# A two-layer attention / S5 diffusion step: the S5 scan tile laid out in runs of 8, x stored early, adaLN steps in pairs, 12 of them moved into S5

## The chip, the core and the metric

The kernel runs on one core of one Trainium2 chip. The metric is the device time of one execution in microseconds. Before the change the median of 3 runs is 2644.32 us (2640.66 to 2646.99). The engines of the core work side by side, each in its own program order: TensorE (PE, with PEld for its weight loads), VectorE (DVE), ScalarE (ACT), GpSimd (POOL) and SyncE (SP, which here only issues transfers).

## The reference, cut

Two token groups (128 context rows `xp`, 128 latent rows `xs`; D = 2048) pass two layers with shared weights. adaLN vectors come from a conditioning vector times a 2048 x 12288 matrix per layer. Layer 0 mixes by attention, layer 1 by a bidirectional diagonal state-space scan (S5) with a gate; a convolutional gated FFN follows each.

```python
for i in range(DEPTH):                      # 2 layers
    mp = ada_params(c_ctx[None, :], ada_w[i], ada_b[i])   # silu(cond) @ w + b, split in 6
    ms = ada_params(c, ada_w[i], ada_b[i])
    hp = rms_norm(xp, norm1_g[i]) * (1 + mp[1]) + mp[0]
    hs = rms_norm(xs, norm1_g[i]) * (1 + ms[1]) + ms[0]
    # i = 0: qkv, attention, w_o      i = 1: s5_mixer
    xp = xp + mp[2] * op; xs = xs + ms[2] * os_
    hp = rms_norm(xp, norm2_g[i]) * (1 + mp[4]) + mp[3]; ...
    xp = xp + mp[5] * conv_ffn(hp, *ffn); ...

def s5_mixer(h, h0, w_in, ..., w_gate, w_out):
    u = h @ w_in                            # 128 groups of 16 channels, 64 states each
    for d, rev in ((0, False), (1, True)):
        bu = einsum('blgc,gpc->blgp', u, bb)        # complex
        hs = associative_scan(abar, bu, reverse=rev)
        y += einsum('blgp,gcp->blgc', hs, c)        # real part
    y = gelu(y); y = y * sigmoid(y @ w_gate)
    return y @ w_out, final states
```

## The kernel before, in words

**Products.** Both token groups stand side by side as two blocks of 128 columns. A weight matrix is streamed from HBM in units of 128 x 1024 float32 (512 KB) by SP into 8 `raw` buffers (a few more in two stretches). A *split* unit is written by ACT as a rounded high part `whi` and by DVE as the remainder `wlo`, up to 3 units ahead; PE then runs 12 matmuls of 512 columns into two `acc` banks (`products`). The first three quarters of w_gate are not split: there PE takes the float32 `raw` directly (`acc<-raw`).

**adaLN steps.** `ada` returns four steps for 512 columns of one adaLN vector. A step takes two units (1 MB) and is four column-tiled float32 matmuls (32 columns of the array each) into the one `ada` bank. The profile records each as two matmuls, so one step is 8 records `ada<-raw,cond`. After the fourth step DVE adds the bias (`adab`, loaded by POOL) into `adaev`, PE transposes it, DVE reduces it to shift or scale columns (or PE and ACT make gate rows). The steps are needed late and are therefore strewn between the dense steps by `spread(main, fill)`, one at a time. 200 steps stand in the program.

**Order.** The program order is made by the code in `run_all`: after each unit `pump()` lets background tasks (attention, convolution, the S5 preparation and scan) put their next instructions into the streams when a planner's clock (`Timeline`) says that their operands are ready. The planner decides the order alone; each engine then runs its stream in order and waits on semaphores. The constants `EARLY` and `FILL` say how many adaLN steps of layer 1 stand in the first FFN (FFN0) and in S5 (in w_in and in the four quarters of w_gate).

**S5.** `w_in` makes u in four quarters q; `s5_prep` (POOL, during FFN0) makes the tables. For each q, `scan_task` multiplies u by the input tables (`ms<-A,A` 128x128), and ACT copies each PSUM bank into the scan tile `SC` (tag S0 for q = 0, 2; tag X for q = 1, 3): 16 copies of 64 x 512. SC holds 33 time steps of 128 values; in one step the values stand as [re/im][group][block]. `steps_task` makes 32 scan steps of 4 DVE instructions each. `out_task` lets ACT copy SC into two tiles `sf` (4 copies of 64 x 2048), PE multiplies these by the output tables (`ms<-A,A` 128x64, column-tiled in halves, 96 records for each of two tiles), ACT applies gelu, PE transposes, ACT copies into y; then the quarter's w_gate products run. Since q = 1 scans in the tile X, where the residual x lives, SP stores x to DRAM (`xd`) first and loads it again at the end.

Of the kernel before, what the change touches and what calls it, by code (L numbers as in the profile page):

```python
# [16 lines left out]
P = 128  # L17
# [20 lines left out]
EARLY = 20  # L38
# [3 lines left out]
FILL = (2, 0, 2, 2, 2)  # L42
# [27 lines left out]
class Timeline:  # L70
# [144 lines left out]
    def engine(self, eng, name, outs, ins, args, kw):  # L215
        n = max(math.prod(x.shape[1:]) for x in outs + ins)
        scal = sum(isinstance(kw.get(k), bass.AP) for k in ("scale", "bias", "scalar1", "scalar2"))
        big = [x for x in ins if math.prod(x.shape[1:]) > 1 or n == 1]
        scal += len([x for x in ins if math.prod(x.shape[1:]) == 1 and n > 1 and not any(x is kw.get(k) for k in ("scale","bias"))])
        if eng == "ACT":  # L220
            ps = self.in_psum(big[0])
            slow = 1.0
            for x in outs + big:
                st = [d for d in list(x.ap)[1:] if d[1] > 1]
                if st and abs(st[-1][0]) > 16: slow = 2.15
            c = (0.05 if ps else 0.095) + slow * n / 1200.0 + 0.09 * scal + 0.09 * ("accum_out" in kw)
# [12 lines left out]
        self.run(eng, c, outs, ins, name)
# [38 lines left out]
def spread(main, fill):  # L278
    out, j = [], 0
    for i, s in enumerate(main):  # L280
        out.append(s)
        while j < len(fill) and (j + 1) * len(main) <= (i + 1) * len(fill):
            out.append(fill[j])
            j += 1
    return out + fill[j:]
# [3 lines left out]
def hybrid_kernel(ctx: ExitStack, tc: tile.TileContext, a):  # L289
# [206 lines left out]
    def run_all():  # L496
# [13 lines left out]
        j = 0  # L510
        for u in units:
# [17 lines left out]
            pump()  # L529
# [816 lines left out]
    class S5:  # L1346
# [43 lines left out]
        def scan_task(self):  # L1390
# [8 lines left out]
            w1 = view(wt, 0, [[64, 2], [2, 32], [1, 2]])  # L1399
            w2 = view(wt, 128, [[64, 2], [2, 32], [1, 2]])  # L1400
            for q in range(4):
# [13 lines left out]
                gps.memset(SC[:, 0, :, :, 0], 0.0)  # L1415
                gps.tensor_copy(SC[:, 0, :, :, 1], s5par["H0"][:, :, 32 * q:32 * q + 32])
                for e2 in range(2):
                    e = 2 * q + e2
                    for h in range(2):
                        for ri in range(2):  # L1420
# [9 lines left out]
                            bw = view(SC, 32 * 128 + ri * 64 + g0, [[1, 16], [-128, 32]], (64, 64))  # L1430
# [6 lines left out]
                a_re = view(s5par["A4"], 32 * q, [[0, 2], [1, 32], [0, 2]])  # L1437
                a_im = view(s5par["A4"], G + 32 * q, [[G, 2], [1, 32], [0, 2]])
# [3 lines left out]
        def steps_task(self):  # L1442
            q = 0
            while q < 4:
# [3 lines left out]
                for s in range(32):  # L1448
                    cur = SC[:, s]
                    swp = view(SC, s * 128 + 64, [[-64, 2], [2, 32], [1, 2]])  # L1450
# [10 lines left out]
        def out_task(self):  # L1461
# [8 lines left out]
            for q in range(4):  # L1470
# [6 lines left out]
                gps.tensor_copy(fin[:, :, 32 * q:32 * q + 32], SC[:, 32, :, :, 0])  # L1477
# [172 lines left out]
    m = s5.w_in()  # L1650
    start_hook(ffn0.last_up, lambda: (spawn(s5.steps_task()), spawn(s5.scan_task()), spawn(s5.out_task())))
# [110 lines left out]
```

## Time and profile before

| | |
|---|---|
| median of 3 runs | 2644.32 us |
| profiled execution, own time | 2647.6 us |
| its span, first to last instruction | 2645.8 us |
| PE busy | 2545.2 us, 96% |
| DVE / ACT / POOL busy | 60% / 50% / 17% |
| TensorE clock granted, mean | 0.987 of full speed |
| chain of work that ended last | PE 86%, ACT 4%, DVE 4%, DMA 3% |
| HBM traffic | 651 MB, mean 246 GB/s |

Stages in the span: adaLN prologue to 24 us, qkv with attention to 389, w_o to 531, FFN0 to 1410, w_in 1417 to 1553, w_gate quarters 0 to 2 to 1725, w_gate quarter 3 and w_out to 1871, FFN1 to the end. An engine that is not the bottleneck may idle at no cost, so the busy share is read stage by stage: where PE never waits, the time of the stage is the sum of its matmuls.

### The profile page before, as it was taken

How to read it: one execution, taken by the hardware profiler on the slowest of the kernel's cores; microseconds unless marked ns; L12 is line 12 of the kernel's file. 1: busy time of each engine (PE TensorE's matmuls, PEld its weight loads, DVE VectorE, ACT ScalarE, POOL GpSimd, SP SyncE). 2: the span in 40 equal slices, each digit the busy share in tenths (PEclk: the TensorE clock that was granted, in tenths of full speed). 3: DMA queues.
4: the chain of work that ended last, by engine and by line, in shares of the span. 5: the costliest groups of instructions: out<-in, count | busy, mean ns of one | idle time of the engine just before them, and what ended most of it. 6: DMA issues, size and time to landing. Idle time of an engine off the chain costs nothing.

```text
span 2645.8 us, 35232 instructions
## 1 busy us (share of the span) xinstructions
PE 2545.2 (96%) x13011; PEld 1893.5 (72%) x13011; DVE 1599.1 (60%) x2370; ACT 1323.0 (50%) x1764; POOL 442.5 (17%) x455
## 2 busy tenths in 40 slices
PE   8999999999999999999998769999999999999998
PEld 4666677667777777777776655466677788888896
DVE  4765554567665665566656386655656565666566
ACT  5333444356554554455455668543555544554354
POOL 0002000011465555455530000000000000000000
PEclk9999999999999999999999889999999999999999
DMA  9979877977888888888886756789677756665663
GB/s 360 321 254 312 295 229 274 365 247 238 263 262 270 272 264 271 263 264 259 275 280 224 220 165 175 218 284 308 221 249 242 242 192 193 186 184 190 191 194 125
DMA packets 388741, 651.11 MB, mean 246 GB/s; under 512 B 81740, under 2 KB 100300, under 8 KB 386648
## 3 DMA queue, kind: packets, MB, share of 16 engines
q1 hardware_dynamic: 364064, 621.10, 71.5%
q10 hardware_dynamic: 20424, 20.47, 3.0%
q0 software_dynamic: 4080, 7.28, 0.9%
q8 instruction: 102, 1.67, 0.3%
q14 instruction: 71, 0.58, 0.1%
HBM read 623.72 MB, written 25.03 MB: 245 GB/s over the span
## 4 chain that ended last, share of the span: by engine, by line
PE 86%; ACT 4%; DVE 4%; DMA 3%; issue 1%; ACTq 1%; POOL 1%; SPq 0%
PE acc L348 73%; PE ada L348 6%; PE ms L361 4%; PE ms L348 3%; ACT A L259 2%; DVE A L259 2%; DVE wlo L259 1%; DMA raw<-in_ada_w_dram 1%; ACT X L259 1%; ACTq L259 1%; ACT whi L259 1%; DMA raw<-in_na_w_o_dram 1%; POOL S L259 1%; ACT S L259 0%; DMA xd<-X 0%
## 5 line engine op out<-in xcount | busy, mean ns | idle before, releaser
L348 PE MATMUL acc<-whi,A 128*128 128x512 f32 (+1 forms) x5536 | 1796.7, 396 | 31.2 <-ACT whi L259 22.4
L259 DVE TENSOR_TENSOR wlo<-raw,whi 128x1024 fp32r<-128x1024 f32 (+2 forms) x697 | 885.8, 1276 | 688.5 <-ACT whi L259 668.8
L348 PEld LDWEIGHTS acc<-whi,A 128*128 128x128 f32 x5536 | 1042.8, 189 | 358.6 <-issue 92.5
L348 PE MATMUL acc<-wlo,A 128*128 128x512 f32 (+1 forms) x2768 | 1080.6, 390 | 11.4 <-DVE wlo L259 10.9
L259 ACT ACTIVATE whi<-raw 128x1024 fp32r<-128x1024 f32 (+2 forms) x697 | 724.5, 1043 | 693.2 <-PE acc L348 557.5
L348 PEld LDWEIGHTS acc<-wlo,A 128*128 128x128 f32 x2768 | 523.2, 189 | 117.7 <-DVE wlo L259 21.0
L259 DVE SCALAR_TENSOR_TENSOR A<-ms,cw,A 128x254 f32<-128x254 f32 x344 | 157.8, 479 | 88.9 <-ACT A L259 80.6
L348 PE MATMUL ada<-raw,cond 128*32 128x512 f32 (+1 forms) x1396 | 196.9, 595 | 6.1 <-DVE adaev L259 4.0
L259 POOL TENSOR_TENSOR S<-S,A 128x512 f32<-128x512 f32 x128 | 182.8, 1448 | 50.3 <-PE ms L361 50.3
L259 POOL DMA_DIRECT2D adab<-in_ada_b_dram x48 | 24.9, 518 | 711.5 <-DVE ada L259 383.6
L259 POOL TENSOR_TENSOR S<-S 128x512 f32<-128x512 f32 (+1 forms) x96 | 132.9, 1384 | 7.5
L259 ACT ACTIVATE A<-ms,cw 128x256 f32<-128x256 f32 x172 | 88.0, 562 | 87.9 <-PE ms L361 87.9
L361 PEld LDWEIGHTS ms<-ident,A 128*128 128x128 f32 (+2 forms) x670 | 80.5, 142 | 47.4 <-ACT A L259 16.2
L361 PE MATMUL ms<-ident,A 128*128 128x128 f32 (+2 forms) x670 | 101.5, 277 | 11.0 <-ACT A L259 10.1
L259 ACT ACTIVATE A<-A 128x512 fp32r<-128x512 f32 (+7 forms) x88 | 72.1, 824 | 66.1 <-DVE A L259 65.5
L259 ACT ACTIVATE A<-ms 128x512 f32<-128x512 f32 (+3 forms) x106 | 55.1, 558 | 96.1 <-PE ms L348 51.0
L348 PE MATMUL ms<-A,A 128*64 128x64 f32 (+1 forms) x1152 | 79.7, 253 | 23.4 <-ACT A L259 19.6
L348 PEld LDWEIGHTS ms<-A,A 128*64 128x64 f32 (+1 forms) x1152 | 75.8, 168 | 35.8 <-ACT A L259 24.2
L259 ACT ACTIVATE S<-ms 128x128 f32<-128x128 f32 (+2 forms) x96 | 58.4, 644 | 70.2 <-PE ms L361 64.5
L348 PE MATMUL acc<-raw,A 128*128 128x512 f32 x192 | 89.3, 614 | 4.3 <-ACT A L259 4.3
L259 ACT ACTIVATE A<-acc 128x512 f32<-128x512 f32 (+1 forms) x112 | 65.2, 588 | 50.4 <-PE acc L348 50.3
L259 POOL DMA_DIRECT2D A<-in_final_g_dram x1 | 0.6, 555 | 504.4 <-ACT whi L259 504.4
(138 smaller groups left out, 1499.0 us busy)
## 6 DMA issues: line engine op xcount, KB each, us to landing
raw<-in_ada_w_dram SPq DMA_DIRECT2D x331, 512.0 KB
raw<-in_ffn_w_up_dram SPq DMA_DIRECT2D x318, 512.0 KB
raw<-in_ffn_w_down_dram SPq DMA_DIRECT2D x168, 512.0 KB
raw<-in_na_w_qkv_dram SPq DMA_DIRECT2D x71, 512.0 KB
raw<-in_s_w_in_dram SPq DMA_DIRECT2D x32, 512.0 KB
raw<-in_s_w_gate_dram SPq DMA_DIRECT2D x32, 512.0 KB
raw<-in_s_w_out_dram SPq DMA_DIRECT2D x32, 512.0 KB
raw<-in_na_w_o_dram SPq DMA_DIRECT2D x28, 512.0 KB
```

What stands on the lines that cost most here:

```text
L259: return fn(*args, **kw)
L348: nc.tensor.matmul(out, lhsT, rhs, **kw)
L361: nc.tensor.transpose(out, in_, ident[:n, :n])
```

## The change

It has four parts.

1. **SC and sf layout.** In one time step SC now holds [re/im][block][group], so 8 groups stand next to each other. The 16 copies in keep their number and size; they write runs of 8 values and read PSUM with a step of 64 values. The copies out become 8 of 64 x 1024 for a q in place of 4 of 64 x 2048, with runs of 8 on both sides. `sf` is [h][re/im][64][8]; the stationary operand of the output matmuls is `sf[:, h, ph, :, s]`, 64 values at a step of 8, where it was 64 contiguous values. The scan's DVE instructions keep count and size.
2. **x to DRAM early.** A hook at the second step of w_in issues both transfers on POOL's queue (`keep_x`); before, SP issued them when q = 1 was reached.
3. **Pairs.** `spread` puts two adaLN steps in a row, and `run_all` pumps after four unsplit units or ahead of a split one, no longer after every unit; so nothing comes between the two steps.
4. **EARLY 20 to 8, FILL (2, 0, ..) to (8, 6, ..).** 12 adaLN steps leave FFN0, 6 enter w_in, 6 the first quarter of w_gate.

```diff
-EARLY = 20
+EARLY = 8
-FILL = (2, 0, 2, 2, 2)
+FILL = (8, 6, 2, 2, 2)
...
 def spread(main, fill):
     out, j = [], 0
     for i, s in enumerate(main):
         out.append(s)
         while j < len(fill) and (j + 1) * len(main) <= (i + 1) * len(fill):
-            out.append(fill[j])
-            j += 1
+            out += fill[j:j + 2]
+            j += 2
     return out + fill[j:]
...
-            pump()
+            run = 0 if u.step.split else (run + 1) % 4
+            if run == 0 or i + 1 == len(units) or units[i + 1].step.split:
+                pump()
...
+        def keep_x(self):
+            self.xd = dt("xd", [P, 2, D])
+            for b in range(2):
+                gps.dma_start(self.xd[:, b], x[b])
...
-                if q == 1:
-                    self.xd = dt("xd", [P, 2, D])
-                    for b in range(2):
-                        sync.dma_start(self.xd[:, b], x[b])
                 um = sb("A2", [P, 16, 2, 2, 32])
-                SC = self.SC[q] = sb(("S0", "X")[q % 2], [P, 33, 2, 32, 2])
+                SC = self.SC[q] = sb(("S0", "X")[q % 2], [P, 33, 2, 2, 32])
...
-                            src = bk.rearrange("p (g c) -> p g c", c=32)
-                            g0 = (e2 * 16 + h * 8) * 2
-                            fw = view(SC, 128 + ri * 64 + g0, [[1, 16], [128, 32]], (0, 64))
+                            src = bk.rearrange("p (g b c) -> p c b g", b=2, c=32)
+                            g0 = e2 * 16 + h * 8
+                            fw = view(SC, 128 + ri * 64 + g0, [[128, 32], [32, 2], [1, 8]], (0, 64))
...
-                sfs = [sb(t, [P, 2, 32, 32]) for t in ("A5", "A12")]
+                sfs = [sb(t, [P, 2, 2, 64, 8]) for t in ("A5", "A12")]
                 for e2, sf in enumerate(sfs):
-                    g0 = e2 * 32
                     yield written(SC, lag=S5_LAG, ahead=AHEAD)
-                    act(sf[0:64], view(SC, g0, [[64, 2], [1, 32], [128, 32]], (0, 64)), AF.Copy)
-                    yield lambda now: tl.t["ACT"] < now + 2.0
-                    act(sf[64:128], view(SC, 31 * 128 + g0, [[64, 2], [1, 32], [-128, 32]], (64, 64)), AF.Copy)
+                    for h in range(2):
+                        g0 = e2 * 16 + h * 8
+                        to = sf[:, h].rearrange("p i (b c) g -> p i b c g", b=2)
+                        act(to[0:64], view(SC, g0, [[64, 2], [32, 2], [128, 32], [1, 8]], (0, 64)), AF.Copy)
+                        act(to[64:128], view(SC, 31 * 128 + g0, [[64, 2], [32, 2], [-128, 32], [1, 8]], (64, 64)), AF.Copy)
...
-                                    mm(o, sf[:, ph, 2 * g:2 * g + 2].rearrange("p b c -> p (b c)"),
+                                    mm(o, sf[:, h, ph, :, s],
                                        ca[e % 2][:, g // 8, ph, :, g % 8], start=ph == 0, stop=False,
                                        tile_position=(0, 64 * h))
...
+    start_hook(m[1], s5.keep_x)
```

The planner's price of an ACT copy with a strided PSUM operand changes too (it is no longer raised); this moves only the order.

**PE, FFN0.** In PE's stream an adaLN step is two rows `ada<-raw` (one for each unit), amid rows of the dense product. Before, one step stands alone:

```order
L348 MATMUL acc_1564_8622<-wlo_8684,A_1448_7899 128x512
L348 MATMUL acc_1564_8622<-whi_8683,A_1448_7899 128x512
L348 MATMUL ada_8541<-raw_8558,cond_92 32x512 x2
L348 MATMUL ada_8541<-raw_8592,cond_92 32x512 x2
L348 MATMUL acc_1589_8774<-whi_8708,A_1199_6327 128x512
```

After, two stand together:

```order
L349 MATMUL acc_1665_9252<-wlo_9392,A_885_4397 128x512
L349 MATMUL acc_1665_9252<-whi_9391,A_885_4397 128x512
L349 MATMUL ada_9177<-raw_9203,cond_92 32x512 x2
L349 MATMUL ada_9177<-raw_9222,cond_92 32x512 x2
L349 MATMUL ada_9177<-raw_9249,cond_92 32x512 x2
L349 MATMUL ada_9177<-raw_9280,cond_92 32x512 x2
L362 MATMUL ms_9471<-ident_65,A_912_4539 128x128 x4
```

In the whole stream the 200 steps stood in 185 groups and now stand in 96. By stage, groups before and after: qkv 52 and 26, w_o 18 and 11, FFN0 72 and 28, the wait for S5's norm 1 and 1, w_in 2 and 4, w_gate 0 to 2 5 and 5, w_gate 3 2 and 2, w_out 14 and 8, FFN1 16 and 8; the 3 of the prologue stay. Steps: qkv 51 and 52, w_o 25 and 24, FFN0 69 and 58, S5's norm 3 and 2, w_in 2 and 8, w_gate 0 to 2 4 and 10; the rest is unchanged.

**DVE, end of w_in.** `A<-S,A4t` and `S<-S,A` are scan steps of q = 0 (two rows a step), the same with X of q = 1; `wlo` are splits, the last of w_in reads raw_12420 before and raw_12554 after. Before:

```order
L259 TENSOR_TENSOR S_2131_12045<-S_2131_12045,A_2128_12042 128x128 x2
L259 TENSOR_TENSOR wlo_12675<-raw_12420,whi_12674 128x1024
L259 TENSOR_TENSOR A_2128_12042<-S_2131_12045,A4t_4707 128x128 x2
L259 TENSOR_TENSOR S_2131_12045<-S_2131_12045,A_2128_12042 128x128 x2
L259 TENSOR_TENSOR A_2128_12042<-S_2131_12045,A4t_4707 128x128 x2
```

After:

```order
L259 TENSOR_TENSOR S_2108_11959<-S_2108_11959,A_2105_11956 128x128 x2
L259 TENSOR_TENSOR wlo_12601<-raw_12502,whi_12600 128x1024
L259 TENSOR_TENSOR adaev_12630<-ada_12363,adab_80 128x512
L259 TENSOR_TENSOR A_2105_11956<-X_12203,A4t_4752 128x128 x2
L259 TENSOR_TENSOR X_12203<-X_12203,A_2105_11956 128x128 x2
```

Before, 10 steps of scan 0 stand behind the last split of w_in; after, scan 0 ends ahead of the last two splits, and scan 1 has begun. Behind scan 1 DVE's stream now has an `adaev` of w_gate's adaLN steps ahead of scan 2.

**POOL, start of w_in.** `xd<-X` stands behind the last products of the S5 preparation:

```order
L259 DMA adab_80<-in_ada_b_dram 2x512
L259 MEMSET S_1040_5340 128x1792
L259 DMA xd<-X_89 128x2048 x2
L259 DMA adab_80<-in_ada_b_dram 2x512
L259 MEMSET S_2108_11959 128x2x32
```

In SP's stream of before the same transfer stood amid the loads of w_in:

```order
L259 DMA raw_12281<-in_s_w_in_dram 128x2x512
L259 DMA xd<-X_89 128x2048 x2
L259 DMA raw_12310<-in_s_w_in_dram 128x2x512
```

## Rows read from the trace of the kernel before

**Rows 1.** The page, busy time of PE: us, share of the span, instructions.
```profile
PE 2545.2 (96%) x13011; PEld 1893.5 (72%) x13011; DVE 1599.1 (60%) x2370; ACT 1323.0 (50%) x1764; POOL 442.5 (17%) x455
```
**Rows 2.** By stage: stretch, length; busy PE PEld DVE ACT POOL; clock, DMA share, GB/s.
```profile
24.00:389.00 365.00, 360.00 (x1842) 251.78 (x1843) 217.89 (x282) 148.81 (x217) 25.87 (x36) 1.00 0.87 295
389.00:531.00 142.00, 137.63 (x727) 93.91 (x726) 69.08 (x88) 58.24 (x97) 4.08 (x8) 0.99 0.88 314
531.00:1410.00 879.00, 870.68 (x4418) 650.65 (x4416) 553.89 (x684) 458.20 (x682) 396.64 (x370) 1.00 0.82 264
1417.00:1553.00 136.00, 117.90 (x552) 92.93 (x552) 76.88 (x168) 77.89 (x86) 0.83 (x3) 0.94 0.65 209
1553.00:1725.00 172.00, 142.08 (x1167) 84.63 (x1165) 117.70 (x439) 116.95 (x89) 2.35 (x9) 0.91 0.66 194
```
**Rows 3.** Timeline, PE, FFN0, one adaLN step: start, us, instruction, count.
```profile
1071.88 0.39 PE L348 MATMUL acc<-wlo,A 128*128 128x512 f32 x1
1072.11 0.40 PE L348 MATMUL acc<-whi,A 128*128 128x512 f32 x1
1072.43 1.07 PE L348 MATMUL ada<-raw,cond 128*32 128x512 f32 x8
...
1073.76 0.39 PE L348 MATMUL acc<-wlo,A 128*128 128x512 f32 x1
```
**Rows 4.** Timeline, PE, w_o, two adaLN steps in a row.
```profile
458.02 0.40 PE L348 MATMUL acc<-whi,A 128*128 128x512 f32 x1
458.35 1.92 PE L348 MATMUL ada<-raw,cond 128*32 128x512 f32 x16
...
460.54 0.39 PE L348 MATMUL acc<-wlo,A 128*128 128x512 f32 x1
```
**Rows 5.** Waits of ACT in qkv, then in w_o: total us, times, longest.
```profile
ACT whi L259 <- DMA raw<-in_na_w_qkv_dram: 44.5, 16, 6.9
...
ACT whi L259 <- DMA raw<-in_na_w_o_dram: 26.1, 11, 8.3
```
**Rows 6.** Timeline, PE, S5; in brackets the idle time before and its releaser.
```profile
1512.75 0.80 PE L348 MATMUL acc<-whi,A 128*128 128x512 f32 x1 [6.84 <-ACT whi L259]
...
1568.53 4.71 PE L348 MATMUL ms<-A,A 128*64 128x64 f32 x96 [14.17 <-ACT A L259]
1576.17 4.35 PE L348 MATMUL ms<-A,A 128*64 128x64 f32 x96 [2.92 <-ACT A L259]
...
1625.41 3.02 PE L348 MATMUL ms<-A,A 128*64 128x64 f32 x96 [2.17 <-ACT A L259]
...
1634.95 1.44 PE L348 MATMUL ms<-A,A 128*128 128x128 f32 x5 [3.69 <-ACT X L259]
```
**Rows 7.** Timeline, ACT, w_in, first copy into X.
```profile
1505.43 1.03 ACT L259 ACTIVATE X<-ms 64x512 f32<-64x512 f32 x1 [7.89 <-DMA xd<-X]
```
**Rows 8.** ACT groups by shape, whole run: count; busy us, mean ns; idle before, releasers.
```profile
L259 ACT ACTIVATE S<-ms 64x512 f32<-64x512 f32 x32 | 33.9, 1060 | 5.7 <-PE ms L348 5.3
...
L259 ACT ACTIVATE S<-S 64x384 f32<-64x384 f32 x64 | 33.0, 516 | 5.0 <-POOL S L259 4.6
...
L259 ACT ACTIVATE A<-S 64x2048 f32<-64x2048 f32 x8 | 30.2, 3780 | 16.1 <-DVE S L259 16.0
...
L259 ACT ACTIVATE A<-A 128x1024 f32<-128x1024 f32 x20 | 21.1, 1054 | 5.1 <-DVE A L259 5.1
...
L259 ACT ACTIVATE A<-ms 128x256 f32<-128x256 f32 x16 | 5.2, 383 | 16.0 <-DMA A<-ld 10.4 <-issue 3.2 <-PE ms L361 1.5
```
**Rows 9.** Groups by shape, 1410 to 1730 us: DVE's scan, PE's output loads.
```profile
L259 DVE TENSOR_TENSOR S<-S,A 128x128 f32<-128x128 f32 x128 | 36.9, 289 | 17.0 <-ACT S L259 14.8
...
L259 DVE TENSOR_TENSOR A<-S,A4t 128x128 f32<-128x128 f32 x128 | 31.5, 287 | 1.7
...
L348 PEld LDWEIGHTS ms<-A,A 128*64 128x64 f32 x768 | 26.1, 152 | 24.2 <-ACT A L259 21.2 <-issue 2.3 <-ACT whi L259 0.8
```
**Rows 10.** Transfers: a load of 1 MB on POOL's queue, us to landing.
```profile
A<-in_final_g_dram POOLq DMA_DIRECT2D x1, 1024.0 KB, 7.1
```

More of the change, by code (lines that the diff above doesn't have):

```diff
@@ L224, in engine @@
                 st = [d for d in list(x.ap)[1:] if d[1] > 1]
-                if st and abs(st[-1][0]) > 16: slow = 2.15
+                if st and abs(st[-1][0]) > 16 and not self.in_psum(x): slow = 2.15
             c = (0.05 if ps else 0.095) + slow * n / 1200.0 + 0.09 * scal + 0.09 * ("accum_out" in kw)
@@ L509, in run_all @@
         ensure_loads()
-        j = 0
-        for u in units:
+        j = run = 0
+        for i, u in enumerate(units):
             if u.step.first:
@@ L1398, in scan_task @@
             self.kt = sb("A10", [P, 2048])
-            w1 = view(wt, 0, [[64, 2], [2, 32], [1, 2]])
-            w2 = view(wt, 128, [[64, 2], [2, 32], [1, 2]])
+            w1 = view(wt, 0, [[64, 2], [32, 2], [1, 32]])
+            w2 = view(wt, 128, [[64, 2], [32, 2], [1, 32]])
             for q in range(4):
@@ L1414, in scan_task @@
                     act(um[:, :, par].rearrange("p r b c -> p r (b c)"), u, AF.Copy, scale=mask_par[:, par:par + 1])
-                gps.memset(SC[:, 0, :, :, 0], 0.0)
-                gps.tensor_copy(SC[:, 0, :, :, 1], s5par["H0"][:, :, 32 * q:32 * q + 32])
+                gps.memset(SC[:, 0, :, 0], 0.0)
+                gps.tensor_copy(SC[:, 0, :, 1], s5par["H0"][:, :, 32 * q:32 * q + 32])
                 for e2 in range(2):
@@ L1426, in scan_task @@
                                    um[:, pr].rearrange("p a b c -> p (a b c)"), start=True, stop=True)
-                            src = bk.rearrange("p (g c) -> p g c", c=32)
-                            g0 = (e2 * 16 + h * 8) * 2
-                            fw = view(SC, 128 + ri * 64 + g0, [[1, 16], [128, 32]], (0, 64))
-                            bw = view(SC, 32 * 128 + ri * 64 + g0, [[1, 16], [-128, 32]], (64, 64))
+                            src = bk.rearrange("p (g b c) -> p c b g", b=2, c=32)
+                            g0 = e2 * 16 + h * 8
+                            fw = view(SC, 128 + ri * 64 + g0, [[128, 32], [32, 2], [1, 8]], (0, 64))
+                            bw = view(SC, 32 * 128 + ri * 64 + g0, [[-128, 32], [32, 2], [1, 8]], (64, 64))
                             act(fw, src[0:64], AF.Copy)
@@ L1436, in scan_task @@
                     yield
-                a_re = view(s5par["A4"], 32 * q, [[0, 2], [1, 32], [0, 2]])
-                a_im = view(s5par["A4"], G + 32 * q, [[G, 2], [1, 32], [0, 2]])
+                a_re = view(s5par["A4"], 32 * q, [[0, 2], [0, 2], [1, 32]])
+                a_im = view(s5par["A4"], G + 32 * q, [[G, 2], [0, 2], [1, 32]])
                 yield written(SC, lag=S5_LAG, ahead=AHEAD)
@@ L1449, in steps_task @@
                     cur = SC[:, s]
-                    swp = view(SC, s * 128 + 64, [[-64, 2], [2, 32], [1, 2]])
+                    swp = view(SC, s * 128 + 64, [[-64, 2], [32, 2], [1, 32]])
                     nxt = SC[:, s + 1]
@@ L1476, in out_task @@
                     fin = view(sb("cw", [P, 4, 86]), 0, [[G, 2], [1, G]])
-                gps.tensor_copy(fin[:, :, 32 * q:32 * q + 32], SC[:, 32, :, :, 0])
-                sfs = [sb(t, [P, 2, 32, 32]) for t in ("A5", "A12")]
+                gps.tensor_copy(fin[:, :, 32 * q:32 * q + 32], SC[:, 32, :, 0])
+                sfs = [sb(t, [P, 2, 2, 64, 8]) for t in ("A5", "A12")]
                 for e2, sf in enumerate(sfs):
-                    g0 = e2 * 32
                     yield written(SC, lag=S5_LAG, ahead=AHEAD)
-                    act(sf[0:64], view(SC, g0, [[64, 2], [1, 32], [128, 32]], (0, 64)), AF.Copy)
-                    yield lambda now: tl.t["ACT"] < now + 2.0
-                    act(sf[64:128], view(SC, 31 * 128 + g0, [[64, 2], [1, 32], [-128, 32]], (64, 64)), AF.Copy)
+                    for h in range(2):
[3 more added lines that the diff above has]
+                        act(to[64:128], view(SC, 31 * 128 + g0, [[64, 2], [32, 2], [-128, 32], [1, 8]], (64, 64)), AF.Copy)
                 self.sc_free[q] = True
```

## The prediction, made before the changed kernel ran

> **What bounds the kernel now.** The page's busy times come first: PE is busy 96% of the span [rows 1], so a change counts if it takes time out of PE's stream or out of PE's waits. The table by stage comes next, and in it the idle time of PE. In FFN0 PE is busy 870.7 of 879 us, in qkv 360.0 of 365 and in w_o 137.6 of 142: there the stage is the sum of PE's instructions. In w_in 18.1 of 136 us are idle and in the quarters 0 to 2 of w_gate 29.9 of 172, and the granted clock falls to 0.94 and 0.91 [rows 2]: there PE waits for S5. The third view is PE's timeline around adaLN steps, for the price of one; the fourth PE's timeline in S5, with each wait's releaser; the last the groups by shape, for the copies that these waits end with. The sum is made against the profiled execution, 2647.6 us, which is 3.3 us over the median; the predicted time is on the median's basis.
>
> **Pairs, the price.** Ordinary products start 0.23 us apart (1071.88, 1072.11). From 1072.11 to 1073.76 there are two ordinary products and one step: 1.65 us, less 0.46 is 1.19 us for a step that stands alone [rows 3]. From 458.02 to 460.54 there are two ordinary products and two steps: 2.52 − 0.46 = 2.06 us [rows 4]. So a further step in a group costs 0.87 us, and a group costs 0.32 us beside its steps. Some groups stand beside a transposition, where less than 0.32 is to be had; I take 0.3 a group. The steps in a row are not cheaper as such: their number stays 200, and only the groups go from 185 to 96.
>
> **Pairs, by stage.** qkv loses 26 groups, 26 × 0.3 = 7.8 us, and gains one step, 0.9: −6.9 where PE is the limit. But qkv's DMA share is 0.87 [rows 2], and ACT's split waited 16 times for a load, 44.5 us in all [rows 5]. Some of that already reaches PE, so part of what PE saves becomes a wait for data. I take −5, between −7.6 and 0. In w_o it is 7 × 0.3 = 2.1 and a step of 0.9, −3.0; the share is 0.88 and ACT waited 11 times, 26.1 us: I take −2, between −4 and 0. In FFN0 44 groups go, 13.2 us, and 11 steps, 11 × 0.87 = 9.6: −22.8, taken as −22.7. Its DMA share is 0.82 and the load falls with the steps (11 MB of 232), so nothing there is late behind PE; −20 to −25. In w_out and FFN1 together 14 groups go, 4.2 us, less 0.9 for a step that lies elsewhere: −3.3. Sum of these: −33.0. Two steps in a row need four buffers of `raw` at once, out of eight; the units behind them then come late for the splits. The splits run up to three units ahead, and PE's 2 us for a pair is the time of some 9 products, so I cost this at nothing in FFN0; in qkv and w_o it is within the bounds above.
>
> **x to DRAM early.** In w_in PE waits 6.84 us for a split [rows 6]. ACT could not make it, since a copy into X stood ahead of it in ACT's stream and waited 7.89 us for the store of x [rows 7]. Issued at w_in's second step, on POOL's queue, the same 1 MB has over 80 us; a load of 1 MB on that queue landed in 7.1 us [rows 10]. The wait goes: −6 (1 us is left to the copies themselves, which stay ahead of the split). POOL's queue is not wanted in that time but for `adab` and the memset of SC, and SP's queue is freed of 1 MB amid w_in's loads.
>
> **SC and sf in runs of 8.** A copy in writes at a step of 512 bytes and takes 1060 ns for 512 values; a copy between contiguous tiles takes 1054 for 1024, one of 384 values in runs of 16 takes 516. The line through the last two gives 0.62 us for 512. A copy that reads PSUM at a step of 128 values takes 383 ns for 256, and the line gives 0.41 [rows 8]: the step on the PSUM side costs nothing. So 64 copies in go from 1.06 to about 0.6 us. A copy out takes 3.78 us for 2048 values [rows 8]; two of 1024 in runs take about 2 × 1.06. ACT saves 64 × 0.46 = 29 us and 16 × 3.78 − 32 × 1.06 = 27 us. ACT is no limit, so only what PE waits for it counts.
>
> By this much PE's waits shrink. The 14.17 us at 1554 to 1568 [rows 6] are the rest of scan 0 and then two copies out, 7.56 us. In the order after, scan 0 ends ahead of the last two splits of w_in and the copies take half: I leave 2 of the 14. Of the waits of 2.92, 2.17 and 3.69 us, which end with a copy of ACT each [rows 6], half goes: −4.4. [...] Against this stands a new wait: DVE's scan of two quarters takes 36.9 + 31.5 us [rows 9], 34 each, the adaLN's `adaev` now stands ahead of scan 2 and more PE work stands between, so I put 8 us for scan 3 coming late (0 to 14, the wait that scan 0 cost).
>
> **Steps into S5.** w_in gets 6 steps, 2 groups more: 6 × 0.87 + 2 × 0.32 = 5.8 us; w_gate's first quarter 6 steps without more groups, 5.2 us. Both are PE work in stages with PE waits, but I take them at full price, since each stands behind a wait, not in it. Their 12 MB are 6 in 136 us (44 GB/s on 209) and 6 in 172 us (35 on 194), below the 295 of qkv [rows 2].
>
> S5 is then −6 − 12 − 4.4 − 6 + 8 + 5.8 + 5.2 = −9.4, and more goes in short waits: PE's idle time of both stages is 48.0 us [rows 2], the five waits named are 29.8 of it, and of the other 18.2, much of it splits and products that wait behind copies of ACT, I take half, −9.1. So S5 is about −18.5; with all 48 us gone it would be −48 − 6 + 11 = −43, and with only the wait for x gone −6 + 11 = +5.
>
> **The sum.** −33.0 − 18.5 = −51.5: 2647.6 − 51.5 = 2596.1, on the median's basis 2592.8. I say 2593.
>
> **A price that is on no row: the stationary operand at a step of 8.** The loads of the 96 output products read 64 contiguous values before and then 64 at a step of 32 bytes. There are 8 such groups, 768 loads in all, of which two thirds (512; the third phase takes another operand) change. A load is recorded at 152 ns [rows 9], and 96 products take 3.02 us, 31 ns each [rows 6]: the loads lie beside each other and beside products. Nothing in the trace shows a load at a step. ACT's write shows what a step does to another engine: about 1.7 times the time at 512 bytes. From below, nothing: 3.02 us a group. From above, a load that is not overlapped: 512 × (152 − 31) ns = +62 us. I take nothing, as 31 ns on a record of 152 leave room, and give the rest to the rivals. [...]
>
> **The rivals.**
> A. *The strided load doubles the output products.* The step of 32 bytes acts on a PE load as on ACT's write, about 1.7 to 2 times. 64 of 96 loads at double time give 5.0 us for 3.02, +2.0 a group, +16 for 8: 2609; where it stretches the scan's chain too, up to 2617. For it: ACT's row. Against it: the overlap. [...]
> B. *S5's waits all go.* If scans and copies stay ahead of PE, the 8 us for scan 3 and the 9 left of other idle time go as well: −17 to −21, about 2574. For it: DVE is busy 117.7 of 172 us in w_gate [rows 2]. Against it: the scans are a chain, 4 × 34 us, with copies and products between.
> C. *DMA is the limit where PE saves.* qkv and w_o give nothing (+7), and S5's 12 MB come late behind their own pairs (+3): 2603. For it: ACT's 44.5 and 26.1 us of waits [rows 5].
> D. *Slower than before.* The strided loads lose their overlap wholly: +62, 2655. It ends slower from about +52 on, 102 ns a load, that is, if little of the 152 ns stays hidden. For it: no trace shows such a load hidden; against it: a load would have to be unable to run ahead only because its operand has a step.
> E. *The change doesn't do what it says*: the order has 96 groups and 58 steps in FFN0, so this is no case for the pairs; for the copies it is that runs of 8 are no faster, +8 to +15 on S5, which lies with A (2601 to 2608).
>
> **How the numbers follow.** Forecast (2580 to 2602) 0.50; A with E (2601 to 2617) 0.25; B (2572 to 2580) 0.13; C (2600 to 2606) 0.08; D 0.03; the remaining 0.01 is near no change. The range 2575 to 2617 takes in A and C, and of B the part from 2575; outside lie D, the last 0.01 and part of B, some 0.1 together, and as much again is left for sizes mis-set on both sides. A measurement here tells about 0.2% (5 us) from no change: faster by more 0.95, the same 0.02, slower 0.03.
>
> **What would show it.** In the trace after: two steps in a row at 2.5 us between ordinary products and 96 groups (pairs); FFN0 at about 856 us; w_in near 133 and no wait of ACT for `xd` (x early); copies in near 0.6 us and out near 1.06 (runs of 8); 96 output products at about 3 us (A wrong) or 5 (A right); w_gate's quarters 0 to 2 near 155, with a wait of PE of about 8 us ahead of scan 3's copies out. It is wrong as a whole if the output products take over 5 us, or if qkv and w_o keep 365 and 142 us while PE's busy time in them falls.

## The result

The changed kernel takes 2600.32 us (median of 4 runs, 2598.33 to 2607.51) against 2645.65 us of the kernel before; the ratio is 0.9837, with a 95% interval of 0.9818 to 0.9856. That is 45 us less; the forecast was 51.5 less, 2593. The profiled execution of the changed kernel took 2607.5 us, the longest of its four, so differences read from the two profiles (40 us) are some us too small.

The page's PE row and the table by stage of the changed kernel, in the order of [rows 1, 2]; a stage ends here where the first dense product of the next one starts, and the rows are qkv, w_o, FFN0, w_in and w_gate 0 to 2:

```profile
PE 2522.2 (97%) x13011; PEld 1923.9 (74%) x13011; DVE 1599.8 (61%) x2370; ACT 1267.9 (49%) x1780; POOL 452.8 (17%) x457
```
```profile
24.20:389.60 365.40, 355.14 (x1889) 258.41 (x1889) 218.39 (x291) 150.72 (x222) 26.73 (x38) 1.00 0.88 302
389.60:527.00 137.40, 134.01 (x720) 95.14 (x720) 69.97 (x94) 60.77 (x100) 3.02 (x6) 0.98 0.93 327
527.00:1382.40 855.40, 841.13 (x4279) 652.65 (x4279) 555.87 (x676) 455.40 (x675) 404.79 (x367) 0.99 0.79 255
1382.40:1540.10 157.70, 137.95 (x841) 108.00 (x841) 112.28 (x309) 81.42 (x111) 3.03 (x9) 0.92 0.74 244
1540.10:1689.30 149.20, 144.15 (x1002) 87.22 (x1003) 83.70 (x304) 62.03 (x91) 4.20 (x12) 0.97 0.77 237
```

The same cut of the kernel before, since [rows 2] cut w_in a little earlier:

```profile
24.20:399.50 375.30, 367.05 (x1896) 254.59 (x1896) 221.13 (x288) 150.83 (x222) 26.93 (x38) 1.00 0.87 293
...
1416.90:1585.60 168.70, 131.25 (x776) 104.68 (x777) 107.58 (x289) 98.88 (x98) 1.53 (x6) 0.90 0.62 199
1585.60:1725.40 139.80, 129.20 (x944) 73.02 (x943) 87.13 (x317) 96.06 (x78) 2.02 (x7) 0.95 0.69 203
```

PE's busy time in w_in and w_gate grew by 21.7 us (260.4 to 282.1), where the 12 moved steps explain 11. That is the first thing to explain. The second is that the two stages together became only 1.6 us shorter, although PE's idle time in them fell by 23.2 us (48.0 to 24.8).

PE's timeline in FFN0 shows a pair: 571.14 to 573.65 is 2.51 us with two ordinary products in it, as [rows 4].

```profile
570.91 0.39 PE L349 MATMUL acc<-wlo,A 128*128 128x512 f32 x1
571.14 0.39 PE L349 MATMUL acc<-whi,A 128*128 128x512 f32 x1
571.46 1.92 PE L349 MATMUL ada<-raw,cond 128*32 128x512 f32 x16
573.31 0.50 PE L349 MATMUL acc<-whi,A 128*128 128x512 f32 x1
573.65 0.40 PE L349 MATMUL acc<-wlo,A 128*128 128x512 f32 x1
```

PE's timeline in S5 of the changed kernel, the waits and the first output products. The 14.17 us wait of [rows 6] has become 2.64 and 1.64; but 190 output products take 10.28 us, where 96 took 3.02, and input products wait 6.41 us for ACT's copies into S, a wait that the kernel before does not have:

```profile
1434.31 1.01 PE L349 MATMUL ms<-A,A 128*128 128x128 f32 x3 [6.41 <-ACT S L259]
...
1519.48 0.50 PE L349 MATMUL ms<-A,A 128*64 128x64 f32 x2 [2.64 <-ACT A L259]
1521.63 10.28 PE L349 MATMUL ms<-A,A 128*64 128x64 f32 x190 [1.64 <-ACT A L259]
...
1582.10 2.94 PE L349 MATMUL ms<-A,A 128*128 128x128 f32 x24 [2.51 <-ACT A L259]
1587.59 1.11 PE L362 MATMUL ms<-ident,A 128*128 128x128 f32 x4 [2.54 <-ACT X L259]
```

The groups by shape of the changed kernel, 1383 to 1730 us (count, busy us, mean ns), for [rows 8, 9]. The copies in went from 1060 to 592 ns, the copies out are 1056; the output products' busy time is 41.2 us, where the same group of before, the last line here, has 27.2:

```profile
L349 PE MATMUL ms<-A,A 128*64 128x64 f32 x768 | 41.2, 269 | 4.3 <-ACT A L259 4.3
L349 PEld LDWEIGHTS ms<-A,A 128*64 128x64 f32 x768 | 40.0, 193 | 9.7 <-ACT A L259 5.7 <-issue 4.0
...
L259 ACT ACTIVATE X<-ms 64x512 f32<-64x512 f32 x32 | 18.9, 592 | 14.7 <-PE ms L349 8.9 <-issue 5.5
...
L259 ACT ACTIVATE A<-X 64x1024 f32<-64x1024 f32 x16 | 16.9, 1056 | 11.8 <-DVE X L259 11.5
```
```profile
L348 PE MATMUL ms<-A,A 128*64 128x64 f32 x768 | 27.2, 238 | 19.3 <-ACT A L259 19.3
```

### The profile page after: what moved, and what is told of

Same layout as the page of the kernel before. It is cut to its first block, busy times and chain, and to the rows that moved or that the text cites. A ratio compares the mean times of both kernels' runs of the same rounds, so it can differ in the third digit from the quotient of the medians.

```text
span 2605.7 us, 35286 instructions
## 1 busy us (share of the span) xinstructions
PE 2522.2 (97%) x13011; PEld 1923.9 (74%) x13011; DVE 1599.8 (61%) x2370; ACT 1267.9 (49%) x1780; POOL 452.8 (17%) x457
## 5 line engine op out<-in xcount | busy, mean ns | idle before, releaser
L349 PE MATMUL ada<-raw,cond 128*32 128x512 f32 (+1 forms) x1408 | 168.9, 591 | 1.5 <-DMA raw<-in_ada_w_dram 1.4
L259 POOL TENSOR_TENSOR S<-S 128x512 f32<-128x512 f32 (+1 forms) x96 | 142.5, 1484 | 7.5
L349 PEld LDWEIGHTS ms<-A,A 128*64 128x64 f32 (+1 forms) x1152 | 89.0, 195 | 26.6 <-issue 9.7
L349 PE MATMUL ms<-A,A 128*64 128x64 f32 (+1 forms) x1152 | 92.6, 274 | 13.7 <-ACT A L259 6.8
L349 PEld LDWEIGHTS ada<-raw,cond 128*32 128x32 f32 x1408 | 37.8, 109 | 82.5 <-issue 75.3
```

Source lines behind the costliest of these rows:

```text
L259: return fn(*args, **kw)
L349: nc.tensor.matmul(out, lhsT, rhs, **kw)
```

## The experiments

All stand against the kernel before, run on the same chip (2644.97 to 2646.21 us median). Lengths of the stages in us, each cut as above, from the profiled execution; the time is the median of all runs. A profiled execution can lie some us beside the median (the changed kernel's 7.2 over it, the contiguous operand's 3.2 under it), so a difference of a few us in one stage is read with care.

| kernel | time | qkv | w_o | FFN0 | w_in | w_gate 0–2 | gate 3 | w_out | FFN1 |
|---|---|---|---|---|---|---|---|---|---|
| before | 2645.65 | 375.3 | 138.2 | 879.2 | 168.7 | 139.8 | 35.9 | 116.3 | 757.5 |
| changed | 2600.32 | 365.4 | 137.5 | 855.4 | 157.7 | 149.2 | 33.9 | 116.8 | 755.3 |
| changed, contiguous operand | 2595.74 | 365.8 | 138.2 | 853.8 | 152.1 | 140.5 | 34.1 | 116.7 | 755.2 |
| changed, step of 4 | 2602.97 | 366.0 | 138.1 | 855.8 | 154.1 | 147.5 | 34.0 | 115.6 | 755.2 |
| changed, step of 2 | 2590.72 | 367.6 | 138.8 | 854.4 | 147.7 | 140.5 | 34.0 | 115.5 | 754.9 |
| changed, x stored late | 2598.18 | 364.8 | 137.9 | 852.5 | 153.1 | 142.4 | 34.1 | 116.3 | 755.4 |
| changed, 12 steps back | 2614.86 | 367.0 | 136.7 | 869.4 | 166.0 | 133.8 | 33.9 | 116.6 | 755.3 |
| changed, single steps | 2637.19 | 374.5 | 136.4 | 871.1 | 155.2 | 155.7 | 36.0 | 116.2 | 758.0 |
| before, layout and early x | 2632.65 | 375.2 | 136.2 | 878.1 | 149.3 | 145.2 | 35.9 | 114.7 | 758.0 |
| before, pairs | 2653.64 | 364.4 | 141.9 | 869.2 | 188.0 | 150.8 | 36.3 | 116.6 | 755.3 |
| before, pairs but in FFN0 | 2652.06 | 366.7 | 140.4 | 880.0 | 173.7 | 151.6 | 34.7 | 115.5 | 755.1 |
| before, pairs outside FFN0 and S5 | 2635.42 | 366.1 | 137.5 | 879.6 | 168.9 | 139.8 | 36.3 | 115.1 | 755.3 |
| before, pairs and 12 steps moved | 2653.76 | 365.5 | 136.7 | 857.7 | 210.7 | 141.5 | 35.2 | 113.9 | 755.2 |
| step of 2, steps in fours | 2686.67 | 395.3 | 152.9 | 855.7 | 154.1 | 150.4 | 36.6 | 133.1 | 773.0 |

### The step of the stationary operand

Three kernels change nothing but how the stationary operand of the output products is read from `sf`, the third also how `sf` is laid out and written; the order of the instructions is the same in all. Contiguous:

```diff
-mm(o, sf[:, h, ph, :, s],
+mm(o, sf[:, h, ph].rearrange("p c g -> p (c g)")[:, 64 * s:64 * s + 64],
```

> The changed kernel with one edit: the 512 strided stationary operands of S5's output products read 64 contiguous values of sf instead of 64 values at a step of 32 bytes. Count, sizes and order of all instructions stay the same; what is left out is the right choice of values, so the scan's output is not the reference's. In the changed kernel the groups of 96 output products take 5.0 us, before 3.02 us at full clock. Theory 1 (the step of the stationary operand costs): the groups fall back to 3.0 us, 8 x 2.0 = 16 us less PE work, and the time falls by 12 to 16 us to about 2585 to 2588 us. Theory 2 (the groups are long for another reason, such as the clock or operands that ACT has only just written): the groups stay at about 5.0 us and the time stays at 2600 us.

A step of 4 values:

```diff
+mm(o, sf[:, h, ph].rearrange("p (a c) g -> p a (c g)", a=2)[:, s // 4, s % 4:256:4],
```

> The changed kernel with the stationary operands of S5's output products read at a step of 4 values (16 bytes) instead of 8 values (32 bytes); the same values are not chosen, so the scan's output is not the reference's, and all else is the same. Theory 1a (a load is slow as soon as each 16 bytes give only one value): groups of 96 as long as in the changed kernel, 5.0 us, time 2600 us. Theory 1b (the price grows with the step): about half the extra, 4.0 us a group, time about 2592 us.

A step of 2 values, with the copies out writing runs of 2:

```diff
+sfs = [sb(t, [P, 2, 4, 2, 64, 2]) for t in ("A5", "A12")]
+to = sf[:, h].rearrange("p k i (b c) g -> p (i b c) k g", b=2)
+mm(o, sf[:, h, s // 2, ph, :, s % 2],
```

> The changed kernel with sf laid out so that the stationary operand is read at a step of 2 values (8 bytes) and ACT's copies out write runs of 2 values instead of 8; it computes all of the reference, in the same order of instructions. Theory 1a: two values in each 16 bytes are enough, groups of 96 take 3.0 us; if ACT's copies then stay at 1.06 us, the time is 12 to 16 us under the changed kernel, about 2585 to 2588 us. Theory 1b: the price grows with the step, 3.3 to 3.5 us a group, about 2588 to 2590 us. If runs of 2 make ACT's copies slow again (1.9 us for 1024 values, as before), some waits of S5 come back and 5 to 10 us of the gain are lost.

The output products by shape, 1383 to 1730 us, contiguous, step of 4 and step of 2, and the copies out of the last:

```profile
L349 PE MATMUL ms<-A,A 128*64 128x64 f32 x768 | 27.5, 236 | 5.1 <-ACT A L259 5.1
```
```profile
L349 PE MATMUL ms<-A,A 128*64 128x64 f32 x768 | 40.6, 268 | 4.3 <-ACT A L259 4.3
```
```profile
L349 PE MATMUL ms<-A,A 128*64 128x64 f32 x768 | 26.5, 230 | 5.1 <-ACT A L259 5.0
...
L259 ACT ACTIVATE A<-X 64x1024 f32<-64x1024 f32 x16 | 18.2, 1135 | 8.7 <-DVE X L259 8.5
```

Theory 1a holds for the price: 41.2 us at a step of 8 and 40.6 at 4, but 26.5 at 2 and 27.5 contiguous. Among these four the price does not grow with the step. The sums hold groups at a lower granted clock too (mean 0.80 from 1521.6 to 1531.9 us of the changed kernel); the group of the third quarter's first 96 products, which waits for nothing (1.00 from 1622.3 to 1627.3 us there), shows the same: a step of 8, of 4, of 2, and contiguous.

```profile
1622.31 4.99 PE L349 MATMUL ms<-A,A 128*64 128x64 f32 x96
...
1618.80 4.93 PE L349 MATMUL ms<-A,A 128*64 128x64 f32 x96
...
1611.32 3.09 PE L349 MATMUL ms<-A,A 128*64 128x64 f32 x96
...
1613.32 3.02 PE L349 MATMUL ms<-A,A 128*64 128x64 f32 x96
```

Of the 14 us of PE work, the end shows less: contiguous is 4.6 us under the changed kernel and 7.2 under the step of 4, the step of 2 is 9.6 and 12.3 us under them; the 12 to 16 us that theories 1 and 1a expected are reached by the step of 2 alone, and only against the step of 4. Part of the saved time turns into waits: in w_in and w_gate the contiguous kernel and the step of 2 have 12.7 and 15.7 us less PE work than the step of 4, and 3.6 and 2.4 us more idle time. The step of 2 computes all and is faster than before, 2590.72 us, ratio 0.9801 (0.9780 to 0.9822); against the changed kernel one of its four runs (2599.86) lies in the other's range. Why the contiguous kernel, whose products cost the same, is 5 us above it is not shown; their ranges overlap. The copies out of the step of 2, in runs of 2, cost 1135 ns in place of 1056.

### Pairs by themselves

The edit to the kernel before:

```diff
-            out.append(fill[j])
-            j += 1
+            out += fill[j:j + 2]
+            j += 2
...
-            pump()
+            run = 0 if u.step.split else (run + 1) % 4
+            if run == 0 or i + 1 == len(units) or units[i + 1].step.split:
+                pump()
```

> The kernel before with pairs alone: two adaLN steps in a row, 96 groups in place of 185, nothing else. Theory P (each group costs 0.3 us beside its steps, and nothing of the saving is lost to data that comes late): 89 x 0.3 = 27 us less, about 2618 us; qkv 10 us shorter in PE's timeline, FFN0 11 us (38 groups). Rival D (qkv and w_o are held by their loads, so that PE's saving turns into waits for data there): FFN0 11 us shorter, qkv and w_o together at most 3 us, in all 15 to 19 us less, about 2628 us.

It is slower than before: 2653.64 us, ratio 1.0034 (1.0023 to 1.0046). Both theories fail on the time. qkv lost 10.9 us and FFN0 10.0, as theory P says, and rival D is wrong on qkv. But w_in grew by 19.3 us and w_gate by 11.0. PE's waits there:

```profile
1474.70 2.07 PE L348 MATMUL ms<-A,A 128*128 128x128 f32 x8 [10.21 <-ACT S L259]
...
1520.26 0.79 PE L348 MATMUL acc<-whi,A 128*128 128x512 f32 x1 [8.30 <-ACT whi L259]
...
1571.16 5.39 PE L348 MATMUL ms<-A,A 128*64 128x64 f32 x96 [25.77 <-ACT A L259]
```

One reason is on POOL. The last instructions of the S5 preparation, in this kernel and then in the kernel before:

```profile
1441.86 2.16 POOL L259 TENSOR_TENSOR S<-S 128x512 f32<-128x512 f32 x1
1444.08 1.60 POOL L259 MEMSET S<- 128x1792 f32 x1
```
```profile
1355.95 1.89 POOL L259 TENSOR_TENSOR S<-S 128x512 f32<-128x512 f32 x1
1357.90 1.60 POOL L259 MEMSET S<- 128x1792 f32 x1
```

The preparation goes forward by a place at each `pump()`, and two steps in a row have one where they had several. In the order, its 16 units stood 13 dense units apart and now 15; in the trace a unit takes 50.2 us in place of 44.2. It ends 86 us later, in w_in. To see whether that is all, FFN0 got its single steps back:

```diff
+            alone = not u.step.split and sum(not v.step.split for v in units[max(0, i - 3):i + 4]) <= 2
+            if run == 0 or alone or i + 1 == len(units) or units[i + 1].step.split:
...
-    steps += spread(f[:30], parts(0, 5)) + spread(f[30:], mods[:-HELD]) + mods[-HELD:]
+    steps += spread(f[:30], parts(0, 5), 1) + spread(f[30:], mods[:-HELD], 1) + mods[-HELD:]
```

> The kernel before with pairs everywhere but in FFN0: 140 groups of adaLN steps in place of 185, FFN0 word for word as before. With pairs everywhere the kernel before was slower by 8 us: its S5 preparation, strewn between the steps of FFN0, ended at 1442 us in place of 1356, and w_in and w_gate waited. Theory PREP (the loss comes from the preparation alone, which gets fewer places in PE's stream when FFN0's steps stand in pairs): w_in and w_gate are as long as before (about 309 us together), and 45 groups x 0.3 = 13 us are saved, about 2632 us. Rival (pairs themselves cost something outside FFN0, such as late loads, or S5 is bound at a fixed point of time whatever PE does): qkv's gain is lost again in w_in, 2640 us or more.

2652.06 us, ratio 1.0027: theory PREP falls as the only cause. The preparation again takes 44.2 us a unit, and still w_in is 5 us and w_gate 12 us longer. What the 5 us in w_in are stays open. ACT's timeline shows a part of w_gate's: two splits of the last quarter stand ahead of the copies out of scan 3 and wait 22.26 us for their load, while the scan has ended at 1699.

```profile
1709.42 1.06 ACT L259 ACTIVATE whi<-raw 128x1024 fp32r<-128x1024 f32 x1 [22.26 <-DMA raw<-in_s_w_gate_dram]
1711.66 1.06 ACT L259 ACTIVATE whi<-raw 128x1024 fp32r<-128x1024 f32 x1 [1.18 <-DMA raw<-in_s_w_gate_dram]
1712.62 11.32 ACT L259 ACTIVATE A<-X 64x2048 f32<-64x2048 f32 x3
```

In the kernel before three of the copies stand ahead of them (start, us, idle before):

```profile
1693.83 11.30 ACT L259 ACTIVATE A<-X 64x2048 f32<-64x2048 f32 x3 [8.00 <-DVE X L259]
1707.61 1.06 ACT L259 ACTIVATE whi<-raw 128x1024 fp32r<-128x1024 f32 x1 [2.48 <-DMA raw<-in_s_w_gate_dram]
```

PE waits 1.60 and 5.44 us for these copies, and for none of them in the kernel before. The units of w_gate's quarters 0 to 2 are not split, so in this kernel, as in the changed one and the one with pairs everywhere, `pump()` comes there after every fourth unit and no longer after every one; whether this or the pairs moved the splits was not separated.

So the next kernel pairs the steps of qkv, w_o, w_out and FFN1 alone, with the order of FFN0 and S5 untouched (`spread(..., 1)` there, and `pump()` after every unit there).

> The kernel before with pairs in qkv, w_o, w_out and FFN1 alone; FFN0, w_in and w_gate keep the single steps and the order of instructions that they had. In the kernel with pairs everywhere but in FFN0 two splits of w_gate's last quarter had moved ahead of ACT's copies out of the last scan and waited 22 us for their load; w_gate was 12 us longer. Theory ORDER (the pairs lost only because they moved other work in w_in and w_gate; with the old order there the saving passes through): 47 groups x 0.3 = 14 us less, about 2631 us, w_in and w_gate together 309 us as before. Rival FIXED (S5's chain ends at a point of time that PE's earlier arrival doesn't move): qkv's gain is lost in w_in again, which grows by 5 to 9 us, about 2640 us.

2635.42 us, ratio 0.9960 (0.9949 to 0.9972). w_in and w_gate are as long as before to 0.2 us, and qkv's 9 us arrive at the end. Theory ORDER holds, with 9.6 us for the 14 expected, and FIXED falls: here what PE saves ahead of S5 passes through S5, the order in it being the old one.

### The moved steps

The edit to the changed kernel:

```diff
-EARLY = 8
-FILL = (8, 6, 2, 2, 2)
+EARLY = 20
+FILL = (2, 0, 2, 2, 2)
```

> The changed kernel with the 12 adaLN steps back in FFN0 (70 steps there in 34 groups, 2 in w_in, 4 in w_gate). Theory PREP: the S5 preparation has the same places as in the kernel before with pairs alone, so it ends near 1440 us, and w_in waits for it: w_in to w_gate 2 take some 30 us longer than the end of FFN0 allows, about 2620 to 2630 us. Rival (a step costs the same in any stage, as the prediction had it): FFN0 +10 us, w_in and w_gate -11 us, 2600 us within 4 us.

2614.86 us, 14.5 us slower than the changed kernel. A step does not cost the same anywhere: FFN0 gets 14 us longer and w_in 8 us longer although it has 6 steps less, w_gate 15 us shorter. The preparation takes 50.4 us a unit and ends at 1441 us, in w_in; in the changed kernel 46.1 us, ending at 1369, before w_in. That fewer paired steps in FFN0 bring the preparation's places in PE's stream closer together fits both pairs of kernels (50.2 and 50.4 us a unit with 12 steps more there, 46.1 without). The theory's size was too high (20 to 30 us).

The counterpart moves the steps in the kernel before with pairs, old layout and old store:

> The kernel before with pairs and with the 12 steps moved into S5, but with the old layout of SC and sf and the old store of x. Pairs alone were 8 us slower than before, pairs with the new layout 31 us faster, pairs with layout and moved steps 45 us faster. Theory HIDE (PE waits for S5 in w_in and w_gate whatever comes before, so steps that are moved there cost nothing and what FFN0 loses is gained): FFN0 24 us and qkv 10 us shorter, w_in and w_gate at most 10 us longer than the 309 us of before, about 2622 us. Rival COPY (with the slow copies the end of S5's chain stays where it is in time, so that what PE saves turns into waits, as with the pairs alone): w_in and w_gate 25 us or more longer, 2640 us or more.

2653.76 us, ratio 1.0038. Its FFN0 is 21 us shorter than before and qkv 10, and w_in is 42 us longer. COPY named the outcome, but not its place: the new wait of PE is one, for the bias addition of an adaLN step, which DVE has in its stream behind all of scan 1. PE's row, then DVE's:

```profile
1562.88 1.08 PE L361 MATMUL ms<-ident,adaev 128*128 128x128 f32 x4 [44.63 <-DVE adaev L259]
```
```profile
1561.42 0.61 DVE L259 TENSOR_TENSOR X<-X,A 128x128 f32<-128x128 f32 x2
1561.95 0.18 DVE L259 TENSOR_REDUCE shift<-ms 128x8 f32<-128x32 f32 x1
1562.05 0.68 DVE L259 TENSOR_TENSOR adaev<-ada,adab 128x512 f32<-128x512 f32 x1
```

In the changed kernel, which differs by the layout and the early store, the planner has put the `adaev` ahead of scan 1:

```profile
1505.97 0.68 DVE L259 TENSOR_TENSOR adaev<-ada,adab 128x512 f32<-128x512 f32 x1
1506.58 0.48 DVE L259 TENSOR_TENSOR A<-X,A4t 128x128 f32<-128x128 f32 x2
```

### Layout, early store and single steps

The kernel before with parts 1 and 2 of the change:

> The kernel before with the new layout of SC and sf and with the early store of x, single adaLN steps at their old places. Theory L (waits of PE for ACT's copies and the store go, 29 us as predicted, and the strided stationary operand takes back 16): about 2632 us, with w_in and w_gate 13 us shorter. Rival (the scan's chain starts when the preparation ends and the copies are not its limit): at most 5 us shorter, or longer by the strided loads, 2640 to 2650 us.

2632.65 us, ratio 0.9950 (0.9933 to 0.9966): theory L, to 1 us; w_in and w_gate are 14 us shorter.

The changed kernel without part 3:

> The changed kernel with single adaLN steps: 184 groups in place of 96, and everything else, the 12 steps in S5 too. Theory P (a group costs 0.3 us): 88 x 0.3 = 26 us more, about 2626 us. Theory PREP says in addition that the preparation runs faster (44 us a unit in place of 46), which gives back a few us if S5 waits for it: 2620 us. Rival D (qkv and w_o are held by their loads): their 33 groups cost nothing, 2615 us.

2637.19 us. Pairs are worth 37 us here, not 26. qkv (9.1) and FFN1 (2.7 for 8 groups) are near what theory P has for them, w_gate is 6.5 us longer, and FFN0 differs by 15.7 us, of which 31 groups at 0.32 are 10; the 448 records `ada<-raw` are as many in both. The waits of PE in FFN0 are alike, and its busy time differs by 14.8.

Most of the other 5 us can be read from the trace: with `pump()` after every unit, a step can be cut in two by a transposition between its units. That happens to 5 steps in FFN0 here, and to none in the changed kernel. A half alone takes as long as a whole step, 1.05 us for 4 records where [rows 3] has 1.07 for 8, so a cut step costs about 1 us more and not 0.32; 5 × 0.7 is some 3 us, an estimate.

```profile
887.74 1.05 PE L349 MATMUL ada<-raw,cond 128*32 128x512 f32 x4
888.72 0.66 PE L362 MATMUL ms<-ident,A 128*128 128x128 f32 x4
889.31 1.05 PE L349 MATMUL ada<-raw,cond 128*32 128x512 f32 x4
890.29 0.50 PE L349 MATMUL acc<-whi,A 128*128 128x512 f32 x1
```

### The early store alone

The edit to the changed kernel:

```diff
-    start_hook(m[1], s5.keep_x)
...
+                if q == 1:
+                    self.xd = dt("xd", [P, 2, D])
+                    for b in range(2):
+                        sync.dma_start(self.xd[:, b], x[b])
```

> The changed kernel with the store of x to DRAM back on SP's queue when the second quarter is reached. Theory X: ACT's first copy into X waits 8 to 9 us for the store again, the splits of w_in behind it are late, and the time rises by 6 us, to about 2606 us. Rival (ACT has so much room with the faster copies, and scan 0 still runs then, that only part of it reaches PE): 0 to 3 us.

2598.18 us (2593.16 to 2599.93): no slower than the changed kernel, so the rival holds. ACT waits for the store as before (5.80 us), but PE has no wait over 1.1 us from 1440 to 1510:

```profile
1465.19 0.59 ACT L259 ACTIVATE X<-ms 64x512 f32<-64x512 f32 x1 [5.80 <-DMA xd<-X]
```

### More than two in a row

In qkv, w_o, w_out and FFN1 `out += fill[j:j + 4]`, on the kernel with the step of 2. `run_all` then pumps after eight unsplit units in place of four, and so also in w_gate's quarters 0 to 2.

> The kernel with the stationary operand at a step of 2 values, and adaLN steps in fours in place of pairs in qkv, w_o, w_out and FFN1 (30 groups there in place of 53, FFN0 and S5 as they are). Theory P alone: 24 groups x 0.3 = 7 us less, 2584 us. Rival BUF (four steps take all 8 raw buffers, so the loads and splits of the dense units behind them come late; the two places where four steps stand in a row today are followed by a wait of PE of 2.6 and 3.5 us): 24 x 2.5 = 60 us more less 7, up to 2640 us where each group shows that wait.

2686.67 us, ratio 1.0158. BUF holds in kind, not in size: 96 us more than the step of 2, where its bound was about 53. PE waits 55.8 us for ACT's splits (18.1 without the fours), in waits of 2 to 3.5 us behind groups of four, and the products behind them take 0.8 us in place of 0.4. PE's busy time is up by 40 us (2502.4 to 2542.3) at a mean granted clock of 0.972 in place of 0.990; BUF had counted the waits alone. w_gate, whose steps did not change, is 9.9 us longer, with the rarer pumps. PE in qkv behind a group of four, then PE's waits for splits in the whole run (us, times, longest):

```profile
247.15 0.79 PE L349 MATMUL acc<-whi,A 128*128 128x512 f32 x1 [2.85 <-ACT whi L259]
248.41 0.80 PE L349 MATMUL acc<-wlo,A 128*128 128x512 f32 x1 [0.46 <-DVE wlo L259]
```
```profile
PE acc L349 <- ACT whi L259: 55.8, 22, 3.5
PE acc L349 <- DVE wlo L259: 18.9, 30, 0.8
```

## Why the prediction was right, and where its steps were not

The time lies in the range, 7 us above the forecast and within its band (2580 to 2602), though rival A (2601 to 2617) is what happened to the output products. That is in part luck: errors of both signs stood in the sum.

- **S5 as a whole**: −18.5 taken, −1.6 measured in w_in and w_gate 0 to 2. Its waits were right in sum: the terms for idle time add up to −23.5 and it fell by 23.2, though with a wait of 6.41 us at 1434 that no term named and without the 8 us for scan 3. Its PE work was wrong: +21.7 us where the clock's −6 and the steps' +11 make +5. Of the 17 us between, 14 are the output products. No run shows the term of 6 us for the clock: the mean granted clock of the two stages went from 0.90 and 0.95 to 0.92 and 0.97, and by this count (21.7 less 11 and 14) some 3 us came back, an estimate; with the step of 2 it is 0.96 and 0.97, and PE's busy time is up by 4.0 us (260.4 to 264.4) where the steps make 11. In the kernel with the step of 4, whose products cost the same and whose profiled execution lies at its median, the two stages are 6.9 us shorter than before, so some 5 us of the miss belong to the changed kernel's profiled execution.
- **What made up for it**: the stages outside gave 36.1 us for 33.0, and w_gate's last quarter 2.0 that the sum did not have.

- **The price of a pair** was right: 2.51 us. What the price left out is the cut step: 6 of FFN0's steps, 3 of qkv's and 2 of w_o's were cut in two before and none is now. **FFN0**: −23.8 measured, −22.7 taken. **w_out and FFN1**: −1.7 for −3.3. **w_o**: −0.8 for −2.
- **qkv**: −9.9 for −5, and 8 to 11 in every paired kernel with pairs of two. I held 2 us back for late loads, and of the 11.9 us by which PE's busy time fell 2.0 did become idle time; ACT's waits for loads stayed at 41.2 us. Rival C, by which qkv gives nothing, is out. The busy time fell by more than the 6.9 priced: 26 groups at 0.32 are 8.3, the 448 records `ada<-raw` and `ada<-A` are as many before and after, and 3 cut steps at 0.7 are 2; between 1 and 2 us stay open.
- **The stationary operand at a step of 8**: taken as nothing, it is rival A, with its size: 5.0 us a group where 3.02 was, +14 us of PE (A had +16). The step that failed is "31 ns on a record of 152 leave room". ACT's row at 512 bytes, 1060 ns where the prediction's line has 620, came nearer. At the end of the kernel it is 5 to 12 us. The prediction's own sign of being wrong as a whole, output products over 5 us, is just met: the groups take 4.99 to 5.22 us.
- **The copies and the waits for them**: 592 and 1056 ns for 0.6 and 1.06; the 14.17 us wait is 4.3 (2 was left). The wait of 8 us for scan 3 did not come; waits of 2.51 us for input products at 1582 and 2.54 for a transposition at 1587 stand in w_gate instead.
- **x early**: −6 taken. The wait behind it went, but in the changed kernel it goes without the early store too: storing late costs nothing measurable there (2598.18 us against 2600.32). That the faster copies are what takes it off PE is likely and not shown by itself. The term was counted beside the copies as if the two were independent.
- **The 12 steps**: taken at full price in both places, near zero in sum, and so as a part that could be left out. It is worth 14.5 us with pairs and layout, and costs 4.5 us (2637.19 against 2632.65) without pairs. What was missing is what FFN0's order does to the S5 preparation, which took 50.4 us a unit with the steps back and 46.1 without them.
- **The sum of parts.** I added the pairs to the layout. Alone they are +8 and −13 us, together −31, with the moved steps −45. Without the layout, pairs in FFN0 and S5 cost more there than they save, by a late preparation, by splits ahead of copies or by an `adaev` behind a scan. The order of the changed kernel was in hand, and it shows `adaev` ahead of scan 1 and scan 0 ending in w_in, so the terms for the waits could be read from it; added up from what each does alone, pairs and layout come to −5 us where together they give −31.

## What to carry to other kernels

Work that is strewn as filler also spaces the background tasks that are pumped around it: before grouping it, look where the tasks' last instruction comes to stand and what waits for it. Prices that are right for an instruction add up only where the order around them stays, so read the order after for each engine in the stage that waits. When a layout is changed for one engine, look at the step that every other engine gets: here two adjacent values for PE's stationary operand gave PE its old speed (26.5 us for 768 output products, 27.2 before) and cost ACT's copies 79 ns of 1056.

## What the runs showed of the hardware

A stationary operand of 64 float32 columns costs nearly the same contiguous and at a step of 8 bytes (27.5 and 26.5 us for 768 products, of which 512 have the step; 3.02 and 3.09 for a group of 96) and half as much again or more at 16 and 32 bytes (40.6 and 41.2; 4.93 and 4.99). ACT's writes in runs of 2 are nearly as fast as in runs of 8 (1135 and 1056 ns for 1024), and its read of PSUM at a step of 64 values shows no price (592 ns for 512, where the prediction's line through two other copies, an estimate, has 620). Half an adaLN step by itself, two of its four column-tiled matmuls, holds PE as long as the whole (1.05 and 1.07 us).
